# Prepared tiles, exponentials, sizes and output weights: where a scheduler may place operations that wait for a load

## The chip, the cores and the metric

The kernel runs on one core of a Trainium2 chip. The metric is device time in microseconds. Five engines work side by side: TensorE (PE in the profile; its weight loads are shown as PEld), VectorE (DVE), ScalarE (ACT), GpSimd (POOL) and SyncE (SP), which here issues nearly all DMA transfers. Each engine takes its instructions in the order in which the program lists them, and waits at an instruction until what that needs is there.

## The reference

One step of a hybrid decoder layer, in float32, for a prompt of 1024 rows and 8 decode sequences of 4 rows, of width 1024:

```
h    = rmsnorm(x, g) * (1 + scale) + shift          # adaLN: scale, shift and gate from silu(c) @ w_ada + b_ada
z    = h @ w_in                                     # split into q,k,v,i,f,o,z of the mLSTM, q,k,v,g of attention, two gates
# mLSTM branch, 4 heads, chunks of 128 rows; C, n, m carried from chunk to chunk
s    = (q k^T) * exp(dmat - m_hat)                  # dmat: causal mask and the cumulated gates
num  = s v + w_inter * (q C);   dot = sum(s) + w_inter * (q n)
h    = num / max(|dot|, exp(-m_hat))
C    = decay * C + (w_end * k)^T v                  # n alike
# attention branch: 8 heads on 2 kv heads, window 128, partial rotary, sinks
# merge by sigmoid gates, y = x + gate * (merged @ w_out), final rmsnorm
```

The outputs are the rows of prompt and samples, and the carried states and caches.

## The kernel before, in words

The large products run on TensorE in blocks of 512 columns, each float32 product as three products of split operands: a rounded weight (`wh_...`, cast by ScalarE) and its remainder (`wl_...`, subtracted by VectorE). Many of them are done in pairs by a scheme of seven products in place of eight, whose sums of weights (`ws`, and sums written back into `wr_ga`, `wr_gm`) VectorE forms ahead of each product. Results are read out of PSUM by VectorE and ScalarE (`gt`, `p`, `by`, `bw`) and stored to device memory (`taD`, `tmD`).

This stream of products is the main work. Between its matmuls a planner (`Side`) places pieces of other streams: the four heads of the mLSTM (`head(h)`), the attention units, the sample heads and the output weights. A piece is placed when its due time on the planner's own clock, `side.now`, has come. The order of TensorE's instructions that results is written down as a chain of order dependencies (`in_order`, with `no_sync`: the later instruction may not be placed before the earlier one, and no semaphore is spent on it).

VectorE and ScalarE are called through the class `Ordered`. While its `on` is true, their order is chained like TensorE's. In the middle part of the kernel, which is where the heads run, `V.on = S.on = False`: there a scheduler places their instructions by a model of its own, subject to true dependencies only. An instruction may then stand ahead of one that was emitted earlier.

A head works on its eight chunks in three groups, `GROUPS = ((0, 1, 2), (3, 4, 5), (6, 7))`, by stages:

- `load(p)`: loads q, k, v of the group (`hq`, `hk`, `hv`), the gate rows (`et<-nmd`) and the carried weights (`qw<-wid`), each broadcast to 128 partitions.
- `prep(p)`: on VectorE, `et += cmask` and `qw *= q`. These wait for the loads.
- `stage_e(p)`: on ScalarE, the exponential of `et`, one operation for each chunk.
- `stage_a(p)`: transposes of k and v (`tk`, `tv`), the scores `S`, and `et *= S`.
- `stage_b(p)`: the outer products `U`, and on VectorE the chain of states `C` (copy, or `C*dec + U`), one for each chunk, in six rotating buffers. `S`, `U` and the numerators `n` share two PSUM buffers.
- `stage_c(p)`: the numerators `n` from `et` and v, `qw` and `C`, copied to `et` by ScalarE, and their squares.
- `stage_f`: the sizes of the eight denominators (`f8den`, one operation for each group), then a chain of small operations for the factors (`f8v`, `f8r_y`, `f8r_w`). `stage_c3` scales `et` by them, `stage_d` transposes it (`ty`).

The output weights come in lots of one k (4, 5, 6, 7) or two (0 and 2, 1 and 3): `out_weights` loads each half (`wor<-w_out`), multiplies it by the gate on VectorE, and stores it (`woDp`, `woDb`) for the last part of the kernel. Nearly all tiles of 128x512 and less (`et`, `qw`, `hq`, `wor`, `wr_...`, `gb`) come from one ring of 50 buffers (`ht`), so a load can have to wait until a store has emptied its buffer.

In the profile all VectorE, ScalarE and GpSimd operations carry line 220 (the helper that calls them), matmuls 259, transposes 264, DMA issues 247. They are told apart by the names of their tiles.

## Time and profile before

| | |
|---|---|
| runs of the kernel | 838.80, 839.07, 839.33 us (median 839.07) |
| profiled execution | 838.28 us |
| its span (first to last instruction) | 836.5 us |
| mean granted TensorE clock | 0.993 |
| busy: PE, DVE, ACT, POOL | 812.5, 595.0, 420.1, 67.4 us |

In the lines below a row of the timeline is: start in us, duration in us, engine, line, operation, tile written and tiles read, shapes, count; in brackets the idle time of the engine just before it and what ended that. Rows with SPq are DMA issues. A row of windows gives for a stretch of time the busy time of PE, PEld, DVE, ACT and POOL with counts, then the granted clock, the DMA engines' busy share, and GB/s. A row of waits gives the total idle time, how often, and the longest. Rows of DMA issues end with the median time from issue to landing.

### The profile page before, as it was taken

How to read it: one execution, taken by the hardware profiler on the slowest of the kernel's cores; microseconds unless marked ns; L12 is line 12 of the kernel's file. 1: busy time of each engine (PE TensorE's matmuls, PEld its weight loads, DVE VectorE, ACT ScalarE, POOL GpSimd, SP SyncE). 2: the span in 40 equal slices, each digit the busy share in tenths (PEclk: the TensorE clock that was granted, in tenths of full speed). 3: DMA queues.
4: the chain of work that ended last, by engine and by line, in shares of the span. 5: the costliest groups of instructions: out<-in, count | busy, mean ns of one | idle time of the engine just before them, and what ended most of it. 6: DMA issues, size and time to landing. Idle time of an engine off the chain costs nothing.

```text
span 836.5 us, 15032 instructions
## 1 busy us (share of the span) xinstructions
PE 812.5 (97%) x5129; PEld 670.9 (80%) x5129; DVE 595.0 (71%) x1479; ACT 420.1 (50%) x1030; POOL 67.4 (8%) x128
## 2 busy tenths in 40 slices
PE   6999999999999999999799999999999999999996
PEld 3779897888788788888688877787788789997775
DVE  4889886656655556475575886797668988974776
ACT  4664365655474564545445454444346654334343
POOL 0120000000000001000001010000002104250000
PEclk9999999999999999999899999999999999999998
DMA  9997766346436335388654354464236785643532
GB/s 337 373 356 233 203 188 201 118 156 210 140 111 196 104 107 174 112 271 292 228 175 167 106 178 138 156 203 141 99 93 191 239 291 180 214 134 131 201 107 108
DMA packets 106689, 153.96 MB, mean 184 GB/s; under 512 B 20448, under 2 KB 54368, under 8 KB 106580
## 3 DMA queue, kind: packets, MB, share of 16 engines
q1 hardware_dynamic: 100964, 142.25, 52.1%
q10 hardware_dynamic: 4176, 6.56, 2.3%
q0 software_dynamic: 1472, 4.20, 1.3%
q8 instruction: 40, 0.66, 0.3%
q14 instruction: 37, 0.30, 0.1%
HBM read 109.22 MB, written 44.75 MB: 184 GB/s over the span
## 4 chain that ended last, share of the span: by engine, by line
PE 91%; DVE 4%; DMA 2%; ACT 1%; issue 1%; SPq 1%; DVEq 0%; ACTq 0%
PE bx L259 11%; PE bw L259 11%; PE by L259 11%; PE g_aq L259 6%; PE bz L259 6%; PE g_w_mo L259 5%; PE g_mq L259 3%; PE foW L259 3%; PE foX L259 3%; PE foY L259 2%; PE smp L259 2%; PE oT L259 2%; PE foZ L259 2%; PE sc L259 2%; PE pt L264 2%; PE g_ak L259 1%
## 5 line engine op out<-in xcount | busy, mean ns | idle before, releaser
L220 ACT ACTIVATE p<-p,nmx 128x256 f32<-128x256 f32 (+1 forms) x64 | 31.0, 485 | 13.0 <-DVE nmx L220 12.7
L259 PE MATMUL g_aq<-h_h,wh_aq 128*128 128x384 f32 (+1 forms) x96 | 32.2, 336 | 0.0
L220 DVE CUSTOM_DVE_ANT_0 p<-sc,cst,sink 128x256 f32<-128x256 f32 (+1 forms) x64 | 26.2, 464 | 6.9 <-PE sc L259 6.8
L259 PE MATMUL g_aq<-h_h,wl_aq 128*128 128x384 f32 (+1 forms) x96 | 30.9, 322 | 0.0
L259 PE MATMUL g_aq<-h_l,wh_aq 128*128 128x384 f32 (+1 forms) x96 | 30.8, 321 | 0.0
L259 PE MATMUL g_w_mo<-ym_l,wh_w_mo 128*128 128x384 f32 (+1 forms) x96 | 30.8, 321 | 0.0
L259 PE MATMUL g_w_mo<-ym_h,wh_w_mo 128*128 128x384 f32 (+1 forms) x96 | 30.8, 321 | 0.0
L259 PE MATMUL g_w_mo<-ym_l,wl_w_mo 128*128 128x384 f32 (+1 forms) x96 | 30.8, 321 | 0.0
L247 POOL DMA_DIRECT2D oD<-uqv x16 | 8.9, 554 | 183.4 <-ACT uqv L220 183.4
L220 ACT ACTIVATE et<-et,an 128x128 f32<-128x128 f32 x32 | 11.2, 397 | 19.5 <-DVE et L220 19.3
L220 DVE COPY p<-pt 128x512 f32<-128x512 f32 (+1 forms) x16 | 10.5, 655 | 13.7 <-PE pt L264 13.7
L259 PEld LDWEIGHTS g_aq<-h_h,wh_aq 128*128 128x128 f32 x96 | 18.0, 188 | 2.6 <-issue 1.5
L259 PEld LDWEIGHTS g_w_mo<-ym_l,wh_w_mo 128*128 128x128 f32 x96 | 18.0, 188 | 0.0
L259 PEld LDWEIGHTS g_aq<-h_l,wh_aq 128*128 128x128 f32 x96 | 18.0, 188 | 0.0
L259 PEld LDWEIGHTS g_w_mo<-ym_h,wh_w_mo 128*128 128x128 f32 x96 | 18.0, 188 | 0.0
L259 PE MATMUL sc<-ukv,uqv 64*128 64x256 f32 (+1 forms) x128 | 18.0, 390 | 0.0
L259 PEld LDWEIGHTS g_w_mo<-ym_l,wl_w_mo 128*128 128x128 f32 x96 | 18.0, 188 | 0.0
L259 PEld LDWEIGHTS g_aq<-h_h,wl_aq 128*128 128x128 f32 x96 | 18.0, 188 | 0.0
L220 DVE TENSOR_TENSOR et<-et,cst 128x384 f32<-128x384 f32 (+1 forms) x12 | 6.1, 512 | 16.5 <-DMA et<-nmd 16.5
L264 PE MATMUL pt<-cst,p 128*128 128x128 f32 x120 | 16.4, 277 | 1.1 <-DVE mx L220 1.1
L259 PE MATMUL g_mq<-h_h,wh_mq 128*128 128x384 f32 (+1 forms) x48 | 16.8, 349 | 0.3 <-ACT mk L220 0.3
L220 ACT ACTIVATE sq<-rows_h 128x512 f32<-128x512 f32 (+2 forms) x14 | 8.2, 582 | 17.7 <-issue 12.0
(2073 smaller groups left out, 2848.0 us busy)
## 6 DMA issues: line engine op xcount, KB each, us to landing
x<-xT SPq DMA_DIRECT2D x16, 256.0 KB, 5.4
early_h<-w_ada SPq DMA_DIRECT2D x8, 512.0 KB, 9.1
adar_ga<-w_ada SPq DMA_DIRECT2D x16, 256.0 KB, 4.0
wr_ga<-w SPq DMA_DIRECT2D x16, 256.0 KB, 2.5
wr_gm<-w SPq DMA_DIRECT2D x16, 256.0 KB, 3.3
taD<-gt SPq DMA_DIRECT2D x16, 256.0 KB, 2.2
tmD<-gt SPq DMA_DIRECT2D x16, 256.0 KB, 4.8
wor<-w_out SPq DMA_DIRECT2D x16, 256.0 KB, 3.9
```

The lines of the kernel that those rows point to most:

```text
L220: ins = f(*args, **kw)
L247: ins = (eng or nc.sync).dma_start(out, in_)
L259: in_order(nc.tensor.matmul(out, lhsT, rhs, start=start, stop=stop, skip_group_check=more))
L264: in_order(nc.tensor.transpose(out, in_, idn))
```

## The change

`Ordered` remembers the instruction it emitted last (`before`). Within `with not_before(engine):`, an operation emitted while the order is not fixed gets an order dependency on that instruction: the scheduler may not place it ahead. It may still place other, later or earlier emitted, operations on either side. Four kinds of operation are put under it: `prep` (24 operations of VectorE, 12 of each kind), `stage_e` (32 exponentials of ScalarE), the sizes of `stage_f` (12 of VectorE) and the multiplies of `out_weights` (16 of VectorE). No operation is added or taken away.

```diff
                 def call(*args, **kw):
                     ins = f(*args, **kw)
+                    i = getattr(ins, "ins", ins)
                     if self.on:
                         in_order(ins, self.name)
+                    elif self.late and self.before is not None:
+                        no_sync(i, [self.before])
+                    self.before = i
                     return ins
                 return call
+
+        @contextmanager
+        def not_before(*engs):
+            for e in engs:
+                e.late = True
+            yield
+            for e in engs:
+                e.late = False
...
-                V.tensor_tensor(et[:, :m], et[:, :m], cmask.unsqueeze(1).to_broadcast((128, m, 128)), op=ALU.add)
-                V.tensor_tensor(qw[:, :m], qw[:, :m], q[:, :m * 128].rearrange("p (c e) -> p c e", e=128), op=ALU.mult)
+                with not_before(V):
+                    V.tensor_tensor(et[:, :m], et[:, :m], cmask.unsqueeze(1).to_broadcast((128, m, 128)), op=ALU.add)
+                    V.tensor_tensor(qw[:, :m], qw[:, :m], q[:, :m * 128].rearrange("p (c e) -> p c e", e=128), op=ALU.mult)
...
-                for i in range(len(GROUPS[p])):
-                    S.activation(et[:, i], et[:, i], AF.Exp, bias=an[:, j0 + i:j0 + i + 1])
+                with not_before(S):
+                    for i in range(len(GROUPS[p])):
+                        S.activation(et[:, i], et[:, i], AF.Exp, bias=an[:, j0 + i:j0 + i + 1])
...
-                for q, cs in enumerate(GROUPS):
-                    size(den[:, cs[0]:cs[-1] + 1], w_[q][:, :len(cs), 128])
+                with not_before(V):
+                    for q, cs in enumerate(GROUPS):
+                        size(den[:, cs[0]:cs[-1] + 1], w_[q][:, :len(cs), 128])
...
-                    V.tensor_tensor(t, t, gb[f], op=ALU.mult)
+                    with not_before(V):
+                        V.tensor_tensor(t, t, gb[f], op=ALU.mult)
```

More of the change, by code (lines that the diff above doesn't have):

```diff
@@ L1 @@
-from contextlib import ExitStack
+from contextlib import ExitStack, contextmanager
 import numpy as np
@@ L213, in __init__ @@
             def __init__(self, eng, name):
-                self.eng, self.name, self.on = eng, name, True
+                self.eng, self.name, self.on, self.late, self.before = eng, name, True, False, None
             def __getattr__(self, op):
```

## The prediction

> **What bounds the kernel now.** I read the page's busy shares and chain first, then the table of what TensorE (PE) waited for, then the stretches in which it stood still.

> ```profile
> PE 812.5 (97%) x5129; PEld 670.9 (80%) x5129; DVE 595.0 (71%) x1479; ACT 420.1 (50%) x1030; POOL 67.4 (8%) x128
> PE 91%; DVE 4%; DMA 2%; ACT 1%; issue 1%; SPq 1%; DVEq 0%; ACTq 0%
> ```

> TensorE is busy 97% of the 836.5 us span and carries 91% of the chain. The change adds no work and leaves TensorE's order as it is (the instruction lists of the two programs agree there, and on GpSimd; only the orders on VectorE, on ScalarE and in the DMA issues differ). So the time moves only by what TensorE waits for, and by the clock it is granted.

> ```profile
> PE xc L259 <- ACT xsq L220: 6.4, 1, 6.4
> PE S L259 <- DVE C L220: 5.5, 1, 5.5
> PE pt L264 <- DVE mx L220: 1.1, 1, 1.1
> ```

> The columns are total us, times and longest. The 6.4 us lie at the start, where the order is still fixed by hand and nothing changes. The other two lie in the middle part, where the order changed: S waits 5.5 us for a C, pt 1.1 us for a row maximum. These are all that the change can remove, apart from the clock.

> **The large wait (head 3, second group of chunks).** VectorE and TensorE in order of time:

> ```profile
> 402.76 0.69 DVE L220 TENSOR_TENSOR wl_pgate__4925<-wr_ga,wh_pgate__4924 128x512 fp32r<-128x512 f32 x1
> 409.50 0.56 DVE L220 TENSOR_TENSOR et<-et,cst 128x384 f32<-128x384 f32 x1 [6.06 <-DMA et<-nmd]
> 410.12 0.56 DVE L220 TENSOR_TENSOR qw<-qw,hq 128x384 f32<-128x384 f32 x1
> 410.60 0.34 DVE L220 SCALAR_TENSOR_TENSOR C<-C,dec,U 128x129 f32<-128x129 f32 x1
> ```

> ```profile
> 404.72 0.39 PE L259 MATMUL n<-C,qw 128*128 128x129 f32 x2
> 405.16 0.38 PE L264 MATMUL tv<-cst,hv 128*128 128x128 f32 x2
> 411.00 1.22 PE L259 MATMUL S<-hq,hk 128*128 128x128 f32 x4 [5.46 <-DVE C L220]
> ```

> TensorE is done at 405.54 (405.16 + 0.38). The next S needs the PSUM buffer of U, which is free once the third C has been formed. That C (it can itself not run before the n at 404.72 is through, since it overwrites a C that n reads) stands on VectorE behind et and qw, and et waits 6.06 us for its load. So S starts at 411.00.

> ```profile
> 408.00:410.00 2.00, 0.00 (x0) 0.00 (x0) 0.50 (x1) 0.00 (x0) 0.00 (x0) 0.72 0.93 304
> 412.00:414.00 2.00, 2.00 (x7) 1.61 (x6) 1.62 (x3) 2.00 (x9) 0.10 (x1) 0.50 0.71 215
> 414.00:416.00 2.00, 2.00 (x6) 1.56 (x6) 1.30 (x3) 0.76 (x2) 0.00 (x0) 0.57 0.57 214
> ```

> In these stretches the third number from the right is the granted clock. 0.72 over 408 to 410 puts the fall to 0.50 at 408.9, and 0.57 over 414 to 416 puts the return at 415.7. TensorE thus worked from 411.0 to 415.7 at half speed, and lost half of 4.7 us: 2.35 us more.

> **Does the change take this wait away?** Not by order. In the changed program the third C still stands behind this et and qw: they are held behind the instruction emitted just ahead, and that is no longer a C. The wait shrinks only if the load lands earlier. Its issue, with what SP did ahead of it:

> ```profile
> 399.15 0.68 DVE L220 TENSOR_TENSOR gt<-p,bw 128x512 f32<-128x512 f32 x1
> 399.87 0.63 ACT L220 ACTIVATE gt<-gt 128x512 f32<-128x512 f32 x1 [3.22 <-DVE gt L220]
> 395.18 0.39 PE L259 MATMUL bw<-h_h,wl_pgate__4696 128*128 128x512 f32 x1
> 396.75 1.29 DVE L220 TENSOR_TENSOR wor<-wor,gb 128x512 f32<-128x512 f32 x2
> 400.53 0.32 SPq L247 DMA_DIRECT2D taD<-gt  x1
> 402.08 0.42 SPq L247 DMA_DIRECT2D hq<-qD  x1
> 403.51 0.42 SPq L247 DMA_DIRECT2D et<-nmd  x1
> woDp<-wor SPq DMA_DIRECT2D x8, 256.0 KB, 3.9
> et<-nmd SPq DMA_DIRECT2D x8, 192.0 KB, 5.0
> ```

> SP issues in order, so the loads stood behind the store of gt. gt's matmuls ended at 395.57, but VectorE came to it only at 399.15, behind four multiplies of output weights that had been hoisted (two in the row at 396.75). In the changed program these four come later, and the two of k=7 (wor71, wor70) stand around gt instead. Step by step:
> - gt can run at 395.6. Its store is issued 1.38 us later, as before (400.53 - 399.15): 397.0.
> - wor70 follows gt, at about 396.2 to 396.9 (two multiplies take 1.29), and its store is issued at about 397.0. All these tiles share a ring of 50 buffers, and by the changed program's waits et's new buffer is the one that this store empties: it lands at the group's median of 3.9 us, so et's load is issued at 400.9 instead of 403.51.
> - et lands 5.0 us later (median): 405.9. From et's start to the end of C it took 1.44 us (410.94 - 409.50), and 0.06 to S: 407.4.
> - TensorE waits 407.4 - 405.54 = 1.9 us instead of 5.46: a gain of 3.6.

> The unknown is the landing. This load's own time before, issue to start of the operation, was 5.99 us (409.50 - 403.51), which leaves a wait of 2.9. At the other end, a load as quick as the hk of the same size

> ```profile
> hk<-kD SPq DMA_DIRECT2D x8, 192.0 KB, 2.8
> ```

> leaves none. I take the median of et's own group, and keep a gain of 2.6 to 5.46.

> The clock fell 3.4 us after the wait began (408.9 - 405.54), so a wait of 1.9 should leave it, and the 2.35 us come back; the bound below is nothing. [...]

> **The small wait (head 1, second group).**

> ```profile
> 286.22 0.56 DVE L220 TENSOR_TENSOR et<-et,cst 128x384 f32<-128x384 f32 x1 [1.31 <-DMA et<-nmd]
> 286.81 0.40 ACT L220 ACTIVATE et<-et,an 128x128 f32<-128x128 f32 x1 [1.06 <-DVE et L220]
> 289.41 0.69 DVE L220 TENSOR_TENSOR wl_phead_in__3654<-wr_mk,wh_phead_in__3653 128x512 fp32r<-128x512 f32 x1 [1.41 <-ACT wh_phead_in__3653 L220]
> 290.97 0.66 PE L264 MATMUL pt<-cst,p 128*128 128x128 f32 x4 [1.11 <-DVE mx L220]
> ```

> et waits for its load, ScalarE's exponential waits for et, the cast of the next weights is late behind it, its remainder (289.41) too, and the maxima that pt needs come behind that. In the changed program et, qw and this exponential all stand behind the maxima and the weights. The chain goes, and with it about 1.1 us (1.06 of ScalarE's wait covers it; 0.7 if the maxima wait for something else).

> **What is put at nothing.** The four sums of sizes per head, 12 operations, no longer run in gaps but all just before the factors that use them. What hides them is the time to the transposes ty. Head 3 is tightest:

> ```profile
> 476.96 0.15 DVE L220 SCALAR_TENSOR_TENSOR f8den<-et 128x2 f32<-128x2 f32 x1
> 477.15 0.17 DVE L220 TENSOR_TENSOR f8den<-f8den,fl 128x8 f32<-128x8 f32 x1
> 481.05 1.35 DVE L220 TENSOR_TENSOR Cs<-Cs,sU 128x387 f32<-128x387 f32 x3
> 483.07 0.68 DVE L220 TENSOR_TENSOR wl_pgate__5792<-wr_gm,wh_pgate__5791 128x512 fp32r<-128x512 f32 x1
> 486.23 0.33 DVE L220 TENSOR_SCALAR et<-et,f8den,f8r_y 128x128 f32<-128x128 f32 x1
> 486.59 0.54 DVE L220 TENSOR_TENSOR vf<-sz,wm 32x387 f32<-32x387 f32 x1
> 494.69 0.71 PE L264 MATMUL ty<-cst,et 128*128 128x128 f32 x5
> ```

> Before, the scaling ended at 486.56, 8.1 us ahead of ty. Now the chain starts behind the Cs sums, at 482.4 at the latest. It has 17 small operations of 0.20 (477.15 - 476.96), 8 scalings of some 0.26, three weight operations of some 0.6, and twelve operations of the sample head that now stand between, of 0.2 to 0.5 (the vf at 486.59 is the longest), together some 4: about 11 us, to 493.4. The cover left is 1.3 us; beyond it, TensorE waits. By the same count heads 0 to 2 keep 3 us or more. The 16 multiplies only feed stores that are read after 700 us. The loads waited for elsewhere cost TensorE nothing before and are asked for later now.

> **The sum,** against the profiled execution's 838.28 us (span 836.5 and 1.8 around it): 3.6 + 2.35 + 1.1 = 7.05, so 831.2. The median of the runs (839.07) is 0.8 above that execution, so I forecast 832.0. Bounds: 2.6 with no clock and 0.7 is 3.3 us (835.8); 5.46 + 2.35 + 1.1 is 8.9 us (830.2).

> **Rivals.** *The load isn't earlier.* C still stands behind et, and if something else on SP holds the loads, the 5.46 and 2.35 stay. For it: SP's queue is long and full of such waits. Against: what held it, gt, was late for a reason that goes. Left is 1.1: 838.0.

> *The wait goes altogether,* when the load lands as hk's do, before 405: 830.2. Against it speak the 5.99 us of this very load. [...] The trace took 7.4 us from hq's issue (402.08) to et.

> *A ring that locks itself (slower).* Before, no load of this group stood behind a store of output weights; now three do (hq, hv and et, behind k=6 and k=7). The store waits for a multiply on VectorE, the multiply stands behind the head's et and qw of the group before, and these wait for their loads, on the same SP. A hold there passes straight on to S, and to every weight load behind it. The load of the group before, and the longest hold of SP near here:

> ```profile
> 388.37 0.38 SPq L247 DMA_DIRECT2D et<-nmd  x1
> 393.31 0.43 DVE L220 TENSOR_TENSOR et<-et,cst 128x256 f32<-128x256 f32 x1 [3.22 <-DMA et<-nmd]
> 406.98 4.85 SPq L247 DMA_DIRECT2D wor<-w_out x3
> ```

> Two holds like the last row's (9.7 us) would make the wait 11.6 us and keep the slow clock: 838.28 + 6.1 - 1.1 is 843.3, with the 0.8 some 844. Up to a hold of 3.6 us the wait stays under that of before; from about 6.4 us the whole kernel is slower by 0.2%. Against it: the et of the group before landed at 393.3, 2.3 us before gt's input was ready (395.57), and nothing that the change does makes it later.

> **How the numbers follow.** Forecast (wait of 1 to 3 us) 0.43, load not earlier 0.20, wait gone 0.17, ring 0.20. A measurement of this kernel can tell about 0.2% (1.7 us) from no change. The load that isn't earlier gives 838.0, within it. So faster 0.62 (0.43 + 0.17, and 0.02 from a load only a little earlier), same 0.19, slower 0.19. The range takes in all cases but the ring: from 829.6, a little under the full gain, to 839.0, a little over the 838.0.

> **What would show it.** Right: S's wait for C between 1 and 3 us, the clock at 1.00 from 405 to 416, pt's wait gone, et's load issued near 401. Wrong: et issued at 403 or later, the clock still at 0.50 there, a wait of ty for the scalings near 494, or TensorE waiting for weight remainders (wl) behind late loads between 360 and 500 us.

## The result, and the profile after

| kernel | executions | median us | lowest to highest | ratio to before (95%) |
|---|---|---|---|---|
| before | 4 | 839.2 | 838.8 to 840.21 | |
| changed | 4 | 834.5 | 832.12 to 835.66 | 0.9939 (0.9915 to 0.9962) |
| changed, again (other runs of before) | 5 | 834.38 | 833.68 to 836.09 | 0.9952 (0.9939 to 0.9965) |

The change makes the kernel faster by 4.7 us by the medians of the first set and by 4.4 us by those of the second. The forecast was 832.0 in a range of 829.6 to 839.0. The profiled execution took 832.12 us (span 830.4); it is the quickest of the nine, and why the others lie up to 4 us above it is a question of its own.

What TensorE waited for in the changed kernel (total us, times, longest; matmuls are on line 271 here, transposes on 276, DMA issues on 259):

```profile
PE xc L271 <- ACT xsq L220: 6.2, 1, 6.2
PE S L271 <- DVE C L220: 2.3, 1, 2.3
...
PE pt L276 <- DVE mx L220: 0.5, 1, 0.5
```

S waits 2.3 us for C instead of 5.5, and pt 0.5 instead of 1.1. Nothing new of more than 0.2 us has come in the middle part. VectorE at the place of the large wait:

```profile
394.72 0.69 DVE L220 TENSOR_TENSOR gt<-p,bw 128x512 f32<-128x512 f32 x1 [0.26 <-PE bw L271]
395.32 0.69 DVE L220 TENSOR_TENSOR wor<-wor,gb 128x512 f32<-128x512 f32 x1
...
404.91 0.56 DVE L220 TENSOR_TENSOR et<-et,cst 128x384 f32<-128x384 f32 x1 [2.33 <-DMA tmD<-gt]
406.11 0.56 DVE L220 TENSOR_TENSOR qw<-qw,hq 128x384 f32<-128x384 f32 x1 [0.64 <-DMA qw<-wid]
406.59 0.34 DVE L220 SCALAR_TENSOR_TENSOR C<-C,dec,U 128x129 f32<-128x129 f32 x1
```

gt now waits for nothing but its own matmuls. The C still stands behind et and qw. The issues of SP:

```profile
396.45 0.39 SPq L259 DMA_DIRECT2D taD<-gt  x1
397.51 0.32 SPq L259 DMA_DIRECT2D hq<-qD  x1
397.88 0.69 SPq L259 DMA_DIRECT2D hk<-kD  x1
398.77 0.32 SPq L259 DMA_DIRECT2D hv<-vD  x1
399.34 0.32 SPq L259 DMA_DIRECT2D et<-nmd  x1
```

The store of gt goes out at 396.45 (400.53 before) and et's load at 399.34 (403.51). TensorE's own work lies 0.9 us earlier here (tv ends at 404.65, before at 405.54), so the load gained 3.3 of these 4.2 us on it. The granted clock over the wait and the work behind it, third number from the right:

```profile
403.00:406.00 3.00, 1.65 (x15) 1.42 (x14) 0.56 (x1) 1.72 (x8) 0.00 (x0) 1.00 0.78 266
406.00:409.00 3.00, 2.02 (x11) 1.75 (x12) 1.84 (x4) 1.28 (x5) 0.10 (x1) 1.00 0.78 269
409.00:412.00 3.00, 3.00 (x40) 2.58 (x42) 1.70 (x3) 1.94 (x5) 0.00 (x0) 1.00 0.73 256
```

It stays at 1.00. Between the two profiled executions 838.28 - 832.12 = 6.2 us are to be explained: S 3.1 (5.46 - 2.33), the clock 2.35, pt 0.6, the first xc 0.2. These make 6.25.

### The profile page after: what moved, and what is told of

Read it like the earlier page. It is cut to its first block, busy times and chain, and to the rows that moved or that the text cites. A ratio compares the mean times of both kernels' runs of the same rounds, so it can differ in the third digit from the quotient of the medians.

```text
span 830.4 us, 15038 instructions
## 1 busy us (share of the span) xinstructions
PE 810.4 (98%) x5129; PEld 669.3 (81%) x5129; DVE 593.8 (72%) x1479; ACT 420.5 (51%) x1030; POOL 67.2 (8%) x128
## 5 line engine op out<-in xcount | busy, mean ns | idle before, releaser
L220 ACT ACTIVATE p<-p,nmx 128x256 f32<-128x256 f32 (+1 forms) x64 | 31.0, 486 | 12.4 <-DVE nmx L220 12.1
L220 DVE CUSTOM_DVE_ANT_0 p<-sc,cst,sink 128x256 f32<-128x256 f32 (+1 forms) x64 | 26.2, 464 | 5.3 <-PE sc L271 5.2
L259 POOL DMA_DIRECT2D oD<-uqv x16 | 8.9, 554 | 183.2 <-ACT uqv L220 161.0
L220 DVE COPY p<-pt 128x512 f32<-128x512 f32 (+1 forms) x16 | 10.5, 657 | 13.6 <-PE pt L276 13.6
L220 ACT ACTIVATE p<-p,den 128x256 f32<-128x256 f32 (+1 forms) x32 | 14.5, 491 | 5.7 <-DVE den L220 5.6
L220 ACT ACTIVATE sq<-rows_h 128x512 f32<-128x512 f32 (+2 forms) x14 | 8.2, 582 | 17.8 <-issue 12.0
L220 DVE TENSOR_TENSOR et<-et,S 128x384 f32<-128x384 f32 (+1 forms) x12 | 6.1, 510 | 15.4 <-PE S L271 12.7
## 6 DMA issues: line engine op xcount, KB each, us to landing
x<-xT SPq DMA_DIRECT2D x16, 256.0 KB, 5.6
adar_ga<-w_ada SPq DMA_DIRECT2D x16, 256.0 KB, 4.0
wr_ga<-w SPq DMA_DIRECT2D x16, 256.0 KB, 2.9
wr_gm<-w SPq DMA_DIRECT2D x16, 256.0 KB, 3.6
taD<-gt SPq DMA_DIRECT2D x16, 256.0 KB, 2.2
tmD<-gt SPq DMA_DIRECT2D x16, 256.0 KB, 5.3
wor<-w_out SPq DMA_DIRECT2D x16, 256.0 KB, 5.1
```

The costliest lines, as they stand in the source:

```text
L220: ins = f(*args, **kw)
L259: ins = (eng or nc.sync).dma_start(out, in_)
```

## The experiments

**The changed kernel again.** It answers where the other executions' time goes.

> The changed kernel as it is. Its profiled execution took 832.1 us, its other runs 834.4 to 835.7. If the landing of single loads differs from one execution to the next, S waits longer here than 2.3 us, or another load's wait shows, of 2 us together; if the difference lies in the clock, a stretch at under 1.00 shows that the first profile lacks. Time about 834.5.

834.38 us (median of 5), and the profiled execution 834.24, 2.1 us above the first one. First its row of the S that waits, then its windows:

```profile
407.72 1.22 PE L271 MATMUL S<-hq,hk 128*128 128x128 f32 x4 [2.91 <-DVE C L220]
```

```profile
406.00:409.00 3.00, 1.28 (x5) 1.28 (x6) 0.84 (x3) 0.18 (x2) 0.10 (x1) 0.74 0.77 292
409.00:412.00 3.00, 3.00 (x10) 2.33 (x10) 1.61 (x3) 2.19 (x5) 0.00 (x0) 0.69 0.75 279
```

S waits 0.6 us longer (2.91), and this time the clock falls. 0.74 over 406 to 409 and 0.69 over 409 to 412 put 3.4 us at half speed (0.26 and 0.31 of 3 us, doubled, are 1.56 and 1.86), from 407.4 to 410.9. TensorE is at work in 3.1 of them (407.72 to 410.9) and loses 1.6. Together 2.2 us: the difference of the two executions (2.1). Both guesses of the expectation were right at once.

**Only the output weights.** `not_before()` with nothing in its brackets holds nothing back; the comments are added here.

```diff
-                with not_before(V):      # prep
+                with not_before():
...
-                with not_before(S):      # stage_e
+                with not_before():
...
-                with not_before(V):      # stage_f
+                with not_before():
```

> Only the multiplies of the output weights are held back; the prepared tiles, the exponentials and the sizes are placed as before. Theory 1 (the prediction's): gt was late on VectorE because of the multiplies hoisted ahead of it, and so were the loads behind its store. Then this part alone gives the large gain: et's load of head 3's second group is issued near 399.5 instead of 403.5, S waits 2.3 us for C instead of 5.5, the clock stays at 1.00 between 400 and 420, and pt's wait of 1.1 us stays. Time: 0.6 us above the whole change, about 835. Theory 2 (the load of the group before, for which VectorE stood still 3.2 us at 393.3, made gt late): that et is still hoisted here, so S waits 5.5 us and the time is that of before, 839.

836.78 us, 0.9974 (0.9964 to 0.9984) of before: under half of the gain.

```profile
393.82 0.43 DVE L220 TENSOR_TENSOR et<-et,cst 128x256 f32<-128x256 f32 x1 [2.76 <-DMA et<-nmd]
395.66 0.42 DVE L220 TENSOR_TENSOR qw<-qw,hq 128x256 f32<-128x256 f32 x1 [1.41 <-DMA qw<-wid]
...
397.67 0.68 DVE L220 TENSOR_TENSOR gt<-p,bw 128x512 f32<-128x512 f32 x1
```

The multiplies are out of the way, but et and qw of the group before are still hoisted: VectorE stands still for their loads until 395.66, and the rest of what was due runs ahead of gt. gt comes at 397.67, between before (399.15) and the whole change (394.72). TensorE's work lies elsewhere in each execution, so the time since gt's own matmuls ended tells more: gt ran 3.58 us after that before, 1.14 here (they ended at 396.53), and 0.04 in the whole change. et's load is issued at 401.68, S waits 3.11 us instead of 5.46, and the clock is down for 6.8 us (408.9 to 415.8), as before. So theory 1 names the larger part of gt's lateness and theory 2 the rest; the clock, which theory 1 had at 1.00, kept much of the gain from showing.

**Only the prepared tiles and the exponentials** (`not_before()` at the sizes and the output weights, as above).

> Only the prepared tiles and the exponentials are held back; the multiplies of the output weights and the sizes are placed as before. Theory 1: the multiplies still stand ahead of gt and wait for their own loads (until 395.6), so S waits 5.5 us, the clock falls to half as before, and only pt's wait shrinks from 1.1 to 0.5 us: 838.6. Theory 2: VectorE no longer stands still for the group before, gt comes early, S waits 2.3 us: about 835.

840.11 us, 1.0016 (1.0007 to 1.0024): slightly slower than before. VectorE, and then TensorE:

```profile
396.51 0.69 DVE L220 TENSOR_TENSOR wor<-wor,gb 128x512 f32<-128x512 f32 x1 [7.21 <-DMA wor<-w_out]
...
400.66 0.68 DVE L220 TENSOR_TENSOR gt<-p,bw 128x512 f32<-128x512 f32 x1
```

```profile
402.55 0.50 PE L271 MATMUL bw<-t2h,wh_pgate__4792 128*128 128x512 f32 x1 [1.83 <-DVE ws L220]
412.63 0.71 PE L271 MATMUL S<-hq,hk 128*128 128x128 f32 x4 [4.38 <-DVE C L220]
```

With et out of the way, the first hoisted multiply stands at the front and waits 7.21 us for its own load. gt is later than before (400.66). The pile behind it now reaches TensorE itself, which waits 1.83 us for VectorE; S waits 4.38. So theory 1 holds in that the multiplies keep gt late, though S waits less than its 5.5 us, and the time is 1.5 us over its 838.6: it had not foreseen TensorE's new wait and the fall of the clock behind it (403.3 to 406.7). This half of the change alone is worse than none.

**All but the exponentials; all but the sizes** (`not_before()` at the one part, the other three kept).

> The change without its part on ScalarE: prepared tiles, sizes and output weights are held back, the exponentials are not. Theory (the exponentials matter, since with prepared tiles later they stand ahead of ScalarE's copies and casts and wait longer): new waits of TensorE for ScalarE's copies or casts of 1 to 3 us in all, 836. Rival (they do nothing beside the rest): 834.4 as the whole change.

> The change without its part on the sizes: prepared tiles, exponentials and output weights are held back. Theory (the sizes are hidden either way): the time of the whole change, 834.4, S waiting 2.3 to 3 us for C. Rival (sizes at the front of VectorE's queue held other work up): slower than the whole change by the 1 us or more that it would then owe to them.

833.68 us, 0.9941 (0.9928 to 0.9955), and 834.19 us, 0.9949 (0.9938 to 0.9961): both the whole change, within the intervals. S waits 3.22 and 2.82 us in their profiled executions, pt 0.5 in both. My theory on the exponentials falls; that on the sizes holds. The two parts that matter are the prepared tiles and the multiplies, and they matter together: -2.0 us for the multiplies alone, +1.3 for the prepared tiles with the exponentials, -4.4 in the whole. No run holds back these two and nothing else.

**Only one C moved, in the kernel before.** If S waits for the C and not for the load, the order alone must do.

```diff
-                        V.scalar_tensor_tensor(Cn, ...)
+                        ci = V.scalar_tensor_tensor(Cn, ...)
                     else:
-                        V.tensor_copy(Cn, Un[:, i])
+                        ci = V.tensor_copy(Cn, Un[:, i])
+                    newest[:] = [getattr(ci, "ins", ci)]
...
-                V.tensor_tensor(et[:, :m], ...)
+                pi = V.tensor_tensor(et[:, :m], ...)
+                no_sync(getattr(pi, "ins", pi), newest)      # the same at qw
```

> The kernel before, with one more order dependency: a head's prepared tiles may not stand ahead of the newest C of the same head. On VectorE this moves one C by two places, ahead of the et and qw that wait for their load; the load itself stays late. Theory (what S waits for is the C behind the late load, not the load): S's wait goes from 5.5 us to under 0.3, the clock stays at 1.00, pt's 1.1 us stays; 839.2 - 5.46 - 2.35 = 831.4. Rival (the late load is needed by TensorE soon anyway): TensorE waits a little later for n or for what stands behind et and qw on VectorE, and the gain is under 3 us: over 836.

835.95 us, 0.9965 (0.9953 to 0.9977). VectorE, TensorE and ScalarE:

```profile
405.31 0.35 DVE L220 SCALAR_TENSOR_TENSOR C<-C,dec,U 128x129 f32<-128x129 f32 x1 [0.88 <-PE n L259]
410.00 0.56 DVE L220 TENSOR_TENSOR et<-et,cst 128x384 f32<-128x384 f32 x1 [4.34 <-DMA et<-nmd]
```

```profile
411.69 0.43 PE L259 MATMUL smpo<-cst,smps 128*128 128x64 f32 x2 [1.20 <-ACT hv L220]
413.56 0.30 PE L259 MATMUL smp<-wr_ga,c 128*32 128x128 f32 x2 [1.44 <-ACT hk L220]
```

```profile
410.59 0.40 ACT L220 ACTIVATE et<-et,an 128x128 f32<-128x128 f32 x1 [7.08 <-DVE et L220]
```

C is done at 405.66 and S's wait is gone. But the load is as late as it was, and 5 us further on TensorE runs into it by another way: on ScalarE the exponential of et stands ahead of the copies of hv and hk and waits 7.08 us. smpo and smp wait 1.20 and 1.44, and the clock falls for 3.4 us (414.1 to 417.5). The theory is right about S's wait, and the rival about the time: the gain is 2.9 us, under its 3, though the load's lateness reaches TensorE through ScalarE and not through VectorE alone. The edit is a little wider than its name: the scheduler also placed one weight operation of VectorE and a few operations of ScalarE, two of the three exponentials of this et among them, otherwise than before.

**The C moved, and the exponentials held back, in the kernel before.**

> The kernel before, with two edits: the C ahead of et and qw as in the run of that alone, and the exponentials of ScalarE held behind the instruction emitted just ahead. Prepared tiles, sizes and output weights are placed as before, so the loads stay late. Theory (with C moved, TensorE's new waits, 1.2 and 1.4 us, came from the exponential that stood on ScalarE ahead of the copies of hv and hk and waited 7.1 us): with the exponentials behind the copies these two waits and the fall of the clock go: 835.95 - 2.6 - 1.7 = 831.6. Rival (the copies are late for another reason, such as the load of hv): the two waits stay, 836.

833.08 us, 0.9937 (0.9925 to 0.9949).

```profile
402.16 0.50 PE L271 MATMUL bw<-t2h,wh_pgate__4792 128*128 128x512 f32 x1 [1.21 <-DVE ws L220]
416.22 0.50 PE L271 MATMUL bx<-h_h,wh_pgate__4924 128*128 128x512 f32 x1 [1.90 <-ACT gt L220]
```

```profile
415.57 0.60 ACT L220 ACTIVATE gt<-bx 128x512 f32<-128x512 f32 x1 [4.96 <-DVE wor L220]
```

The waits of smpo and smp are gone, as the theory said, and the clock stays at 1.00. But the late loads show at other places, and the time is 1.5 us over the forecast 831.6. bx waits 1.90 us for a gt of ScalarE, which waited 4.96 us for VectorE, where the work piled up behind et. bw waits 1.21 us for a sum of weights of VectorE, which stands behind the et, qw and multiplies that waited for their loads, as in the run of the prepared tiles and exponentials. Here the orders moved the price of the late loads on and took only a part of it.

**The C moved, in the changed kernel** (the same edit, here with the loads early).

> The changed kernel, with one more order dependency: a head's prepared tiles may not stand ahead of the newest C of the same head. On VectorE this moves one C of head 3 by two places, ahead of the et and qw that wait for their loads. Theory (what is left of the change's cost is S waiting for that C, 2.3 and 2.9 us in the two profiled executions, and in one of them 3.4 us at half clock behind it): S's wait goes to under 0.3, the clock stays at 1.00 from 400 to 420, and with it most of the spread between executions goes: 834.4 - 2.6 - about 1 = 830.8. Rival (the late loads show again, as the waits of smp and smpo for hk and hv did when C was moved in the kernel before): waits of 1 to 3 us and the clock's fall stay, 833 or more.

829.78 us, 0.9897 (0.9885 to 0.9910): faster than before and than the changed kernel. The waits of TensorE, then its windows:

```profile
PE xc L271 <- ACT xsq L220: 6.4, 1, 6.4
PE sty L276 <- DVE gs L220: 1.1, 2, 0.8
...
PE pt L276 <- DVE mx L220: 0.5, 1, 0.5
```

```profile
403.00:406.00 3.00, 3.00 (x25) 2.85 (x24) 0.35 (x1) 1.33 (x7) 0.00 (x0) 1.00 0.92 193
406.00:409.00 3.00, 3.00 (x15) 2.44 (x13) 2.27 (x5) 2.70 (x9) 0.10 (x1) 1.00 0.80 303
```

S no longer waits at all, TensorE is busy through the whole stretch, and nothing new shows up. Here only that C has another place: the orders on TensorE and ScalarE are those of the changed kernel. The profiled execution (829.84) is 2.3 us under the changed kernel's first, which is S's wait there, and 4.4 under its second, which is the wait (2.9) and the clock (1.6). The four executions lie within 0.4 us (829.45 to 829.84), where the nine of the changed kernel spread over 4. So the spread came from this wait, through its length and through the clock behind it.

## Why the prediction was right or wrong

- *Not by order, but by an earlier load:* right. C stayed behind et and qw; et's load was issued 4.2 us earlier, and S's wait fell to 2.33 us, forecast 1.9.
- *What made gt late:* the larger part. I named the four multiplies. They alone, held back, brought gt from 3.58 us behind the end of its matmuls to 1.14; the rest is the et and qw of the group before, for whose loads VectorE stood still, and which I had not counted. With only those two kinds and the exponentials held back, gt was later still (400.66), since a multiply then waits at the front. The whole change moves both, which is why the step's number (gt at 395.6, measured 394.72 in a stretch that is 0.9 us earlier) came out.
- *Issue and landing:* issued at 399.34 where I had 400.9. 0.9 us of this is that all of TensorE's work lies earlier; the rest fits the stores of output weights, whose buffers the loads take: they landed in 3.3 us (median of the three here), where I took 3.9. The load was used 5.57 us later where I took 5.0, close to this load's 5.99 before.
- *From et to the end of C:* mis-sized. I took 1.44 us from the old row; it was 2.02 (406.93 - 404.91), because qw's load came 0.64 us after et was done. Before, qw followed et without a wait.
- *The wait in sum:* 2.33 us where I had 1.9. Against TensorE's work the load went out 0.7 us sooner than I thought, landed 0.6 later, and C took 0.6 longer. That the errors nearly cancel is luck; in the second profiled execution they did not (2.91).
- *The clock:* the step that failed. From the one fall of before, 3.4 us after the wait began, I reasoned that a wait under 3.4 us leaves the clock, and booked 2.35 us as gained. Waits of 2.33, 2.82 and 3.22 us did leave it; waits of 2.91 and 3.11 did not, nor did one of 1.83 (prepared tiles and exponentials held back), after which the clock was down from 403.3 to 406.7. In the rows of the last section it goes with how much of the wait fell into one step of 3.41 us. In the first profiled execution a border of these steps, at 405.82, cut the wait into 1.16 and 1.17 us; in the second 2.62 of its 2.91 us fell into one step, and the clock fell. On that reading it was luck that the 2.35 us came back in the first.
- *The sum:* I had 831.2 for a profiled execution. The first took 832.12, mainly 0.4 more of S's wait and 0.5 of pt's. The second took 834.24: 1.0 of S's wait, 0.5 of pt's, 1.6 of the clock. The other seven left no trace. The clock is not the reason in all of them: the one of 834.40 us had a mean granted clock of 0.999, and a fall of 3.4 us to half speed takes 0.002 from the mean of 832 us. What made that one 2.3 us longer than the first is open; a longer wait of S is likely, since the executions agree once that wait is gone.
- *The small wait:* 0.6 instead of 1.1. VectorE's maxima now wait for the scores themselves:

```profile
289.26 0.48 DVE L220 CUSTOM_DVE_ANT_0 p<-sc,cst,sink 128x256 f32<-128x256 f32 x1 [0.62 <-PE sc L271]
289.67 0.48 DVE L220 CUSTOM_DVE_ANT_0 p<-sc,cst,sink 128x256 f32<-128x256 f32 x1
```

  With the second pass over 0.4 us later, pt is late by 0.51 however early VectorE is free. I had allowed for that only in the bound of 0.7.
- *The sizes:* put at nothing, and nothing. Head 3's scaling ended at 485.34 and its transposes began at 488.50 in the changed kernel, a cover of 3.2 us where I had counted 1.3:

```profile
483.71 1.63 DVE L220 TENSOR_SCALAR et<-et,f8den,f8r_y 128x128 f32<-128x128 f32 x6
```

```profile
488.50 1.03 PE L276 MATMUL ty<-cst,et 128*128 128x128 f32 x8
```

- *The rivals:* the loads were earlier. The wait did not go altogether; the group's five loads took 8.6 us from the first issue (397.51) to the use of the last (qw at 406.11), and et's own was used 5.57 us after its issue, where this rival had the 2.8 us that hk's loads took to land (median). The ring did not lock: SP held hk for 0.69 us and hv until 398.77, and passed on.

## What to carry to other kernels

On VectorE an operation that waited for a load held up what stood behind it (6.06 us for et in the kernel before, with the C behind it), and the harm went round: a wait for loads ahead of gt delayed a store's input (gt ran 3.58 us after its matmuls ended), the store stood ahead of the next loads on SP (issued at 400.53, et's load at 403.51), and these stood at the front of the same engine again. Look for what the waiting tensor is holding up (one C of 0.34 us) and move that first; then look for the reason why the load is late, since moving the order alone passed a part of the wait on to the next users here (smpo and smp, 1.20 and 1.44 us). Price such a wait with the clock beside it, as a cost that can come in one execution and not in another: behind the 2.91 us of the one profiled execution the clock took 1.6 us more, behind the 2.33 us of the other nothing. And see whether the executions spread: 832.12 to 836.09 us with this wait in the changed kernel, 829.45 to 829.84 without.

## What the runs showed of the hardware

In the middle part the clock's falls lasted 3.4 us (changed kernel again; C moved in the kernel before; twice in the run of the prepared tiles and exponentials) or about 6.8 us (before, 408.9 to 415.7; only output weights, 408.9 to 415.8), and nothing between. They began up to 0.9 us after TensorE had resumed: in the run of prepared tiles and exponentials S resumed at 412.63 and the second fall shows in these two windows, from 413.5 on:

```profile
412.00:415.00 3.00, 2.37 (x9) 1.96 (x10) 2.25 (x6) 1.62 (x5) 0.00 (x0) 0.75 0.75 263
415.00:418.00 3.00, 3.00 (x11) 2.39 (x10) 1.92 (x4) 0.52 (x1) 0.00 (x0) 0.68 0.68 238
```

The clock's record in the trace gives the changes more closely. Before, its first entry lies at 12.93 us of the span, at full speed; the fall comes 395.946 us after that and lasts 6.827 us, and another fall comes at 832.13. In steps of 3.413 us (half of the 6.827) these are 116, 2 and, for the last from the first entry, 240 steps. In the changed kernel the first entry lies at 9.87 and the one fall, at 825.66, 239 steps behind it. In the run of the prepared tiles and exponentials the two falls begin at 403.28 and 413.52, three steps apart. The steps laid over TensorE's idle time, counted from the first entry (before, changed) or from the run's own falls (the others), where this argument's waits lie:

| run | step of 3.41 us (us of the span) | TensorE idle in it (us) | clock in the next step |
|---|---|---|---|
| before | 405.46 to 408.88 | 3.34 | 0.50 |
| changed | 402.40 to 405.82, and the next | 1.16 and 1.17 | 1.00 |
| changed, again | 404.01 to 407.42 | 2.62 | 0.50 |
| only output weights | 405.53 to 408.94 | 2.44 | 0.50 |
| prepared tiles and exponentials | 399.87 to 403.28 | 1.84 | 0.50 |
| prepared tiles and exponentials | 406.69 to 410.11 | 1.86 | 1.00 |
| prepared tiles and exponentials | 410.11 to 413.52 | 2.52 | 0.50 |
| C moved, kernel before | 410.70 to 414.12 | 2.42 | 0.50 |
